# Low-part score and gate products on all 128 rows, with the low part written into both partition halves

## Chip, cores and metric

One NeuronCore of one Trainium2 chip runs the whole program in one launch. The metric is the device time of a launch in microseconds (us); lower is better. Engines: TensorE (PE, with its weight loads as PEld), VectorE (DVE), ScalarE (ACT), GpSimd (POOL) and SyncE (SP), which issues the DMAs. A line number such as L341 is a line of the kernel before; in the changed kernel the same statements stand two to four lines higher.

## The reference, cut to what matters

A two-layer decoder trunk on 512 tokens of width 1024, all in float32. Each layer has a hybrid mixer, a cross-attention into 256 memory tokens and a SwiGLU FFN. The two places of the mixer that matter here are the scores of branches A and C and the gates of branch B:

```python
s = jnp.einsum('bqhcd,bkhcd->bhcqk', qblk, k)          # branch A: 4 heads x 2 components of 64
s = jnp.einsum('bpnqhd,bpnkhd->bpnhqk', qb, kk)        # branch C: 8 heads of 64
gates = jnp.einsum('bsnc,gncd->gbsnd', xb, gate_w)     # branch B: 16 blocks of 64 x 64, two gates
```

In each the contraction runs over 64 channels.

## The kernel before

The matrix products run in fp32r, a float32 that carries fewer bits in a product. So a tensor is split into a high part (a cast) and a low part (the tensor minus its high part), and a product becomes high x high + low x high + high x low, three matmuls. The main weight products (L810 to L812 and L839 to L841) do this with 128 x 512 moving columns and contraction over all 128 rows, 24 matmuls to a step.

For the 64-channel contractions the kernel stacks two of these products in one matmul. `rope_item` makes, for a pair of 64-channel components (rows 0 to 63 and 64 to 127 of one tile), a Q tile `st[:, c, :]` that holds component c's high part in **both** partition halves (its second half is copied by two DMAs, L583 and L584), and a K tile that holds the high part in component c's own half and the low part in the other half (L587, L588). One matmul over 128 rows (L340) thus gives Qhigh x Khigh + Qhigh x Klow. The Q low part `ql` is one [128, 512] tile with each component in its own half (L581, L582), and its product (L341) uses the 64 rows of that half alone. The gates of branch B (`b_item`) are built the same way: `xs` is the high part in both halves (DMAs of L519 and L520), `gws` holds high and low gate weights, L524 runs over 128 rows and L525 over 64 rows with the low part `xl` (made on POOL, L517 and L518).

A layer has 4 head pairs in A and 4 in C. Each has one Q item and one K item of `rope_item`, and 4 query blocks of 128 queries; a query block has two score groups, each L340 then L341, whose moving width is 128, 256, 384 or 512. A layer has 8 gate items n = 0 to 7, each with two products of L524 and two of L525.

The order of the work is the order in which the program is written out: the loop at the end of the kernel emits one main step after another. Before each step `advance` moves every waiting generator (`rope_item`, `attn_a`, `attn_c`, `b_item`, `gelu_item`) on to its next `yield`, and `refill` and `flush` issue the casts and subtractions (L267 on ACT, L274 mostly on DVE) that split weight chunks needed some steps later. Every engine works its queue in that order, so an instruction that waits holds back all that is behind it on its engine. In layer 2 the four A heads follow one another as consecutive steps; in layer 1 two heads stand ahead of the V product and two behind it. Weight chunks, high and low parts share a pool of [128, 1024] tiles (`a4`, 39 buffers); [128, 512] tiles share `t2` (16 buffers).

Of the kernel before, what the change touches and what calls it, by code (L numbers as in the profile page):

```python
# [12 lines left out]
F32R = mybir.dt.float32r  # L13
AF = mybir.ActivationFunctionType
ALU = mybir.AluOpType
AX = mybir.AxisListType

P = 128
D = 1024
S = 512  # L20
# [33 lines left out]


def make_program():
    """Order of the matrix products: the weight chunks and the steps that use them.

    A chunk is [128, 1024] floats: (weight, layer, first row tile, row tiles, first column, columns).
    """  # L60
    chunks, steps = [], []

    def ch(name, l, k0, nk, c0, nc_):
# [3 lines left out]
    def tile_step(name, l, c0, act, post, n0=0, n1=S, **kw):  # L67
        c = ch(name, l, 0, KT, c0, P)
        st = Step("a", [c], act=act, post=post, nk=KT, ncol=P, off=0, n0=n0, n1=n1, **kw)
        steps.append(st)  # L70
        return st
# [11 lines left out]
    for l in range(L):  # L83
# [39 lines left out]
        for n in range(KT):  # L123
            st = tile_step("w_in", l, OFF_RX + P * n, "x", ("rx", l, n))
# [49 lines left out]
def kernel(  # L174
# [13 lines left out]
    nc = tc.nc  # L188
    chunks, steps = make_program()
# [3 lines left out]
    big = ctx.enter_context(tc.tile_pool(name="big", bufs=1))  # L193
# [4 lines left out]
    def nm(s):  # L198
        count[0] += 1
        return "%s_%d" % (s, count[0])  # L200

    def a4(s, shape, dt=F32):
        return big.tile([P] + shape, dt, tag="a4", name=nm(s), bufs=39)

    def t2(s, width=S):
        return big.tile([P, width], F32, tag="t2", name=nm(s), bufs=16)

    def t2r(s):
        return big.tile([P, S], F32R, tag="t2", name=nm(s), bufs=16)

    def small(s):
        return big.tile([P, 16], F32, tag="sm", name=nm(s), bufs=24)
# [1 line left out]
    def bank(s="ps"):  # L214
        return psp.tile([P, 512], F32, tag="bank", name=nm(s), bufs=8)

    def f(ap):
        return ap.bitcast(F32)

    V, A, G, T = nc.vector, nc.scalar, nc.gpsimd, nc.tensor  # L220
# [115 lines left out]

    def scores(sc, qk, c, i, w):
        qh, ql, kk = qk
        r = slice(64 * c, 64 * c + 64)
        T.matmul(sc[:, :w], qh[:, c, i * P:(i + 1) * P], kk[:, c, :w], start=True, stop=False)  # L340
        T.matmul(sc[:, :w], ql[r, i * P:(i + 1) * P], kk[r, c, :w], start=False, stop=True)  # L341

    def attn_a(l, h, i, qk):
        w = (i + 1) * P
# [162 lines left out]
    def b_item(l, n):  # L507
        xc = bt.pop(("xc", n))
        u, w = slice(0, 64), slice(64, P)
        gws = acts["gw"][n // 4]  # L510
        yield
        xs = a4("xs", [2, S], F32R)
        A.copy(xs[u, 0, :], xc[u])
        A.copy(xs[w, 1, :], xc[w])
        yield
        xl = t2r("xl")
        G.tensor_tensor(xl[u], xc[u], f(xs[u, 0, :]), ALU.subtract)  # L517
        G.tensor_tensor(xl[w], xc[w], f(xs[w, 1, :]), ALU.subtract)  # L518
        nc.sync.dma_start(f(xs[w, 0, :]), f(xs[u, 0, :]))  # L519
        nc.sync.dma_start(f(xs[u, 1, :]), f(xs[w, 1, :]))  # L520
        yield
        z = [bank("z0"), bank("z1")]
        for b, r in enumerate((u, w)):
            T.matmul(z[b], gws[:, n % 4, b, :], xs[:, b, :], start=True, stop=False)  # L524
            T.matmul(z[b], gws[r, n % 4, b, :], xl[r], start=False, stop=True)  # L525
        tr, ti = t2("tr"), t2("ti")
        A.activation(tr[u], z[0][u], AF.Tanh, scale=0.5, bias=hb[u, l, n:n + 1])
        A.activation(ti[u], z[0][w], AF.Tanh, scale=0.5, bias=hb[w, l, n:n + 1])
        A.activation(tr[w], z[1][w], AF.Tanh, scale=0.5, bias=hb[w, l, 8 + n:9 + n])
        A.activation(ti[w], z[1][u], AF.Tanh, scale=0.5, bias=hb[u, l, 8 + n:9 + n])  # L530
        yield
        if n % 2 == 0:
            bt["m"] = a4("m", [2, S])
        mp = bt["m"]
        a, m = t2("a"), mp[:, n % 2, :]
        A.activation(a, tr, AF.Exp, scale=nsp4[:, l, n:n + 1], bias=nsp4[:, l, n:n + 1])
        A.activation(tr, tr, AF.Tanh, scale=sp4[:, l, n:n + 1], bias=sp4[:, l, n:n + 1])
        A.activation(m, a, AF.Square)
        V.scalar_tensor_tensor(ti, ti, 1.0, xc, ALU.add, ALU.mult)
        yield  # L540
        V.scalar_tensor_tensor(m, m, 1.0, tr, ALU.add, ALU.mult)
        bt[("s", n)] = (a, ti, m)
        if n % 2 == 0:
            return
        yield
        A.activation(mp, mp, AF.Sqrt, scale=0.25)
        yield
        for k in (n - 1, n):
            a, ti, m = bt[("s", k)]
            G.tensor_tensor(ti, ti, m, ALU.mult)  # L550
        yield
        for k in (n - 1, n):
            a, ti, m = bt.pop(("s", k))
            V.tensor_tensor_scan(m, a, ti, 0.0, ALU.mult, ALU.add)
            V.scalar_tensor_tensor(m, bt.pop(("ge", k)), 0.5, m, ALU.mult, ALU.mult)
            A.copy(act_of("oB", k)[0], m)
        yield
        for k, m in zip((n - 1, n), (mp[:, 0, :], mp[:, 1, :])):
            dh, dl = act_of("oB", k)
            G.tensor_tensor(dl, m, f(dh), ALU.subtract)  # L560
            mark("oB%d" % l)
# [3 lines left out]
    def rope_item(ps, l, br, h, which):  # L565
        raw, sh = t2("raw"), t2("sh")
        A.copy(raw, ps)  # L567
        V.stream_shuffle(sh, ps, [(j + 8) % 16 if j < 16 else j for j in range(32)])
        tab = acts["tabs", 0]
        G.tensor_tensor(raw, raw, tab[:, 0, :], ALU.mult)  # L570
        G.tensor_tensor(sh, sh, tab[:, 1, :], ALU.mult)
        yield
        st = a4("qk" + br, [2, S], F32R)
        a, b = slice(0, 64), slice(64, P)
        V.tensor_tensor(raw, raw, sh, ALU.add)
        A.copy(st[a, 0, :], raw[a])
        A.copy(st[b, 1, :], raw[b])
        yield
        if which == 0:
            ql = t2r("ql")  # L580
            V.tensor_tensor(ql[a], raw[a], f(st[a, 0, :]), ALU.subtract)  # L581
            V.tensor_tensor(ql[b], raw[b], f(st[b, 1, :]), ALU.subtract)  # L582
            nc.sync.dma_start(f(st[b, 0, :]), f(st[a, 0, :]))  # L583
            nc.sync.dma_start(f(st[a, 1, :]), f(st[b, 1, :]))  # L584
            store[br, h] = (st, ql)
            return
        V.tensor_tensor(st[b, 0, :], raw[a], f(st[a, 0, :]), ALU.subtract)  # L587
        V.tensor_tensor(st[a, 1, :], raw[b], f(st[b, 1, :]), ALU.subtract)  # L588
        qk = store.pop((br, h)) + (st,)
        if h == 0:  # L590
            new_act("o" + br, 4)
        make = attn_a if br == "A" else attn_c
        launch = [(br, make(l, h, i, qk)) for i in range(NT)]
        if done.get("v%s%d" % (br, l), 0) < NT:
            store.setdefault("wait" + br, []).extend(launch)
        else:
            arriving.extend(launch)
# [266 lines left out]
    for k in range(2):  # L864
        c = slice(512 * k, 512 * (k + 1))
        xh, xl = (t[:, k, :] for t in acts["x"][0])
# [157 lines left out]
```

## Time and profile before

| what | value |
|---|---|
| median of 3 runs | 2272.38 us (2271.61 to 2273.64) |
| span of the profiled execution | 2272.3 us |
| PE busy | 2238.5 us (99%) |
| PE weight loads busy | 1821.5 us (80%) |
| DVE busy | 1267.1 us (56%) |
| ACT busy | 898.3 us (40%) |
| POOL busy | 351.6 us (15%) |
| mean granted TensorE clock | 0.991 of full speed |

Matmuls are pipelined and the record of one is longer than the time until the next one starts, so 99% busy doesn't mean that PE is at its peak. What a matmul costs is read from start to start.

### The profile page before, as it was taken

The page shows a single profiled execution, that of the slowest core. Times are in us where ns is not written, and L with a number is a line of the kernel's source. Part 1 is how long each engine was busy: PE and PEld are TensorE (multiplying, and loading weights), DVE is VectorE, ACT ScalarE, POOL GpSimd, SP SyncE. Part 2 cuts the span into 40 slices and gives each one's busy share as a digit, 9 for nine tenths or more (in the row PEclk, how much of TensorE's full clock was granted, in tenths as well). Part 3 has the DMA queues.
Part 4 walks back from the last instruction along what each step waited for, and adds up shares of the span by engine and source line. Part 5 has one row for each costly group of instructions (what it writes and reads, how often), then busy time and mean ns, then how long its engine had stood idle before and what let it go on. Part 6 is the DMA issues. An engine that isn't in the chain of part 4 may idle for free.

```text
span 2272.3 us, 26789 instructions
## 1 busy us (share of the span) xinstructions
PE 2238.5 (99%) x10516; PEld 1821.5 (80%) x10516; DVE 1267.1 (56%) x2058; ACT 898.3 (40%) x1583; POOL 351.6 (15%) x238
## 2 busy tenths in 40 slices
PE   9999999999999999999999999999999999999998
PEld 7778777778888888888887777777788888888887
DVE  6656766646655743243566476666467457332434
ACT  5444466644244332122134445666432342221330
POOL 2202213320300300000022031133203003000000
PEclk9999999999999999999999999999999999999999
DMA  7122323234332222142231222232343323222321
GB/s 269 63 65 76 101 66 97 93 98 166 102 112 102 93 91 86 66 147 100 81 126 56 65 75 93 65 107 84 116 148 105 110 101 103 85 82 97 125 93 38
DMA packets 65278, 224.37 MB, mean 99 GB/s; under 512 B 7936, under 2 KB 7936, under 8 KB 65152
## 3 DMA queue, kind: packets, MB, share of 16 engines
q1 hardware_dynamic: 65152, 222.66, 29.5%
q8 instruction: 83, 1.36, 0.2%
q14 instruction: 43, 0.35, 0.0%
HBM read 212.14 MB, written 2.10 MB: 94 GB/s over the span
## 4 chain that ended last, share of the span: by engine, by line
PE 72%; issue 17%; DVE 5%; POOL 3%; ACT 2%; DMA 0%; SPq 0%; POOLq 0%; ACTq 0%
PE ps L810 17%; PE ps L811 17%; PE ps L812 17%; PE ps L839 5%; PE ps L841 5%; PE ps L840 5%; POOL wlo L274 2%; PE sc L341 2%; PE o L414 1%; PE sc L340 1%; DVE x L482 1%; POOL ln L477 1%; PE tp L408 1%; PE o L370 1%; ACT whi L267 1%
## 5 line engine op out<-in xcount | busy, mean ns | idle before, releaser
L810 PE MATMUL ps<-xh,whi 128*128 128x512 f32 (+1 forms) x1792 | 697.3, 389 | 2.9 <-ACT xh L868 1.7
L811 PE MATMUL ps<-xl,whi 128*128 128x512 f32 (+1 forms) x1792 | 689.1, 385 | 0.8 <-DVE xl L754 0.5
L812 PE MATMUL ps<-xh,wlo 128*128 128x512 f32 (+1 forms) x1792 | 688.2, 384 | 1.3 <-POOL wlo L274 1.3
L274 DVE TENSOR_TENSOR wlo<-raw,whi 128x1024 fp32r<-128x1024 f32 x347 | 447.3, 1303 | 47.7 <-ACT whi L267 40.2
L267 ACT CAST whi<-raw 128x1024 fp32r<-128x1024 f32 x371 | 382.7, 1046 | 148.9 <-PE ps L840 97.8
L810 PEld LDWEIGHTS ps<-xh,whi 128*128 128x128 f32 x1792 | 339.4, 189 | 80.7 <-issue 6.5
L812 PEld LDWEIGHTS ps<-xh,wlo 128*128 128x128 f32 x1792 | 339.2, 189 | 68.9 <-POOL wlo L274 2.1
L811 PEld LDWEIGHTS ps<-xl,whi 128*128 128x128 f32 x1792 | 339.5, 189 | 66.1 <-DVE xl L869 1.0
L477 POOL TENSOR_TENSOR ln<-ln,expo 128x1 f32<-128x1 f32 x24 | 34.4, 1434 | 1082.9 <-DVE ln L476 1082.9
L839 PE MATMUL ps<-whi,hh 128*128 128x512 f32 x352 | 137.1, 389 | 0.0
L841 PE MATMUL ps<-whi,hl 128*128 128x512 f32 x352 | 137.0, 389 | 0.0
L840 PE MATMUL ps<-wlo,hh 128*128 128x512 f32 x352 | 136.9, 389 | 0.0
L744 ACT CAST hh<-fg 128x512 fp32r<-128x512 f32 x44 | 27.3, 620 | 191.8 <-DVE fg L743 191.8
L501 ACT CAST xh<-tp 128x256 fp32r<-128x256 f32 x80 | 28.0, 376 | 178.4 <-PE tp L495 101.2
L733 DVE SCALAR_TENSOR_TENSOR fg<-fg,ps 128x512 f32<-128x512 f32 x44 | 30.3, 688 | 116.9 <-ACT fg L732 116.9
L743 DVE TENSOR_TENSOR fg<-fg,ps 128x512 f32<-128x512 f32 x44 | 30.3, 688 | 114.4 <-PE ps L812 114.4
L570 POOL TENSOR_TENSOR raw<-raw,tabs 128x512 f32<-128x512 f32 x32 | 42.6, 1332 | 250.6 <-ACT raw L567 250.6
L732 ACT ACTIVATE fg<-ps 128x512 f32<-128x512 f32 x44 | 26.3, 598 | 135.2 <-PE ps L812 135.2
L680 DVE SCALAR_TENSOR_TENSOR x<-ps,x 128x512 f32<-128x512 f32 x48 | 33.0, 686 | 80.5 <-PE ps L841 80.4
L274 POOL TENSOR_TENSOR wlo<-raw,whi 128x1024 fp32r<-128x1024 f32 x24 | 63.5, 2661 | 88.4 <-ACT whi L267 88.4
L840 PEld LDWEIGHTS ps<-wlo,hh 128*128 128x128 f32 x352 | 66.1, 188 | 13.7
L839 PEld LDWEIGHTS ps<-whi,hh 128*128 128x128 f32 x352 | 66.1, 188 | 13.7
(233 smaller groups left out, 3576.6 us busy)
## 6 DMA issues: line engine op xcount, KB each, us to landing
raw<-in_wts_dram SPq DMA_DIRECT2D x371, 512.0 KB, 3.6
xs<-xs SPq DMA_DIRECT2D x32, 128.0 KB, 2.2
lng<-in_lnp_in_dram SPq DMA_DIRECT2D x6, 512.0 KB, 4.7
lnb<-in_lnp_in_dram SPq DMA_DIRECT2D x6, 512.0 KB, 5.0
tabs<-in_tabs_in_dram SPq DMA_DIRECT2D x4, 512.0 KB, 8.5
x<-in_x_in_dram SPq DMA_DIRECT2D x4, 512.0 KB, 9.3
qkA<-qkA SPq DMA_DIRECT2D x16, 128.0 KB, 2.2
qkC<-qkC SPq DMA_DIRECT2D x16, 128.0 KB, 2.2
```

The lines of the kernel that those rows point to most:

```text
L267: A.copy(h, raw)
L274: eng.tensor_tensor(lw, raw, f(h), ALU.subtract)
L341: T.matmul(sc[:, :w], ql[r, i * P:(i + 1) * P], kk[r, c, :w], start=False, stop=True)
L477: G.tensor_tensor(st[:, 15:16], st[:, 14:15], expo, ALU.pow)
L570: G.tensor_tensor(raw, raw, tab[:, 0, :], ALU.mult)
L680: V.scalar_tensor_tensor(xs, ps, co, xs, ALU.mult, ALU.add)
L810: T.matmul(pv, wh, xh, start=(kt == 0), stop=False)
L811: T.matmul(pv, wh, xl, start=False, stop=False)
L812: T.matmul(pv, wl, xh, start=False, stop=(kt == st.nk - 1))
L839: T.matmul(ps, xh, wh, start=(i == 0), stop=False)
L840: T.matmul(ps, xh, wl, start=False, stop=False)
L841: T.matmul(ps, xl, wh, start=False, stop=(i == n - 1))
```

## The change

The low parts get the layout of the high parts. `ql` and `xl` become [128, 2, 512] tiles of the `a4` pool, with each component's low part in both partition halves, and the second matmul of each pair (L341, L525) runs over all 128 rows, so that it also multiplies the low part with the low part of K or of the gate weight. The low parts are written with four subtractions of [64, 512] in place of two; those of `xl` move from POOL to DVE. The DMAs that copy the high part are now issued ahead of the subtractions in the program. The pool `a4` has 42 buffers, and a scratch area for dynamic DMAs is made smaller.

```diff
     def a4(s, shape, dt=F32):
-        return big.tile([P] + shape, dt, tag="a4", name=nm(s), bufs=39)
+        return big.tile([P] + shape, dt, tag="a4", name=nm(s), bufs=42)
...
     def scores(sc, qk, c, i, w):
         qh, ql, kk = qk
-        r = slice(64 * c, 64 * c + 64)
         T.matmul(sc[:, :w], qh[:, c, i * P:(i + 1) * P], kk[:, c, :w], start=True, stop=False)
-        T.matmul(sc[:, :w], ql[r, i * P:(i + 1) * P], kk[r, c, :w], start=False, stop=True)
+        T.matmul(sc[:, :w], ql[:, c, i * P:(i + 1) * P], kk[:, c, :w], start=False, stop=True)
...
-        xl = t2r("xl")
-        G.tensor_tensor(xl[u], xc[u], f(xs[u, 0, :]), ALU.subtract)
-        G.tensor_tensor(xl[w], xc[w], f(xs[w, 1, :]), ALU.subtract)
         nc.sync.dma_start(f(xs[w, 0, :]), f(xs[u, 0, :]))
         nc.sync.dma_start(f(xs[u, 1, :]), f(xs[w, 1, :]))
+        xl = a4("xl", [2, S], F32R)
+        for r in (u, w):
+            V.tensor_tensor(xl[r, 0, :], xc[u], f(xs[u, 0, :]), ALU.subtract)
+            V.tensor_tensor(xl[r, 1, :], xc[w], f(xs[w, 1, :]), ALU.subtract)
         yield
         z = [bank("z0"), bank("z1")]
-        for b, r in enumerate((u, w)):
+        for b in range(2):
             T.matmul(z[b], gws[:, n % 4, b, :], xs[:, b, :], start=True, stop=False)
-            T.matmul(z[b], gws[r, n % 4, b, :], xl[r], start=False, stop=True)
+            T.matmul(z[b], gws[:, n % 4, b, :], xl[:, b, :], start=False, stop=True)
...
         if which == 0:
-            ql = t2r("ql")
-            V.tensor_tensor(ql[a], raw[a], f(st[a, 0, :]), ALU.subtract)
-            V.tensor_tensor(ql[b], raw[b], f(st[b, 1, :]), ALU.subtract)
             nc.sync.dma_start(f(st[b, 0, :]), f(st[a, 0, :]))
             nc.sync.dma_start(f(st[a, 1, :]), f(st[b, 1, :]))
+            ql = a4("ql", [2, S], F32R)
+            for w in (a, b):
+                V.tensor_tensor(ql[w, 0, :], raw[a], f(st[a, 0, :]), ALU.subtract)
+                V.tensor_tensor(ql[w, 1, :], raw[b], f(st[b, 1, :]), ALU.subtract)
...
-    nc = _bacc.Bacc("TRN2", target_bir_lowering=False, num_devices=1)
+    nc = _bacc.Bacc("TRN2", target_bir_lowering=False, num_devices=1, dynamic_dma_scratch_size=2048)
```

On PE, ACT and SP the same instructions stand in the same order before and after; on PE the 160 matmuls that were 64 rows high are 128 rows high. DVE has 96 more instructions and POOL 32 fewer.

DVE in the A heads of layer 2, at the second Q item, before (the statement L575 that follows belongs to the K item of the same head, the L350 rows to the first query block of the first head):

```order
L568 STREAM_SHUFFLE sh_9127<-ps_9095 128x512
L581 TENSOR_TENSOR ql_9132<-raw_9033,qkA_9091 64x512
L582 TENSOR_TENSOR ql_9132<-raw_9033,qkA_9091 64x512
L575 TENSOR_TENSOR raw_9079<-raw_9079,sh_9080 128x512
L350 ISA pr_9142,st_9141<-sc_9144,tabs_8747 128x128
```

and after:

```order
L565 STREAM_SHUFFLE sh_9161<-ps_9129 128x512
L581 TENSOR_TENSOR ql_9168<-raw_9065,qkA_9125 64x512
L582 TENSOR_TENSOR ql_9168<-raw_9065,qkA_9125 64x512
L581 TENSOR_TENSOR ql_9168<-raw_9065,qkA_9125 64x512
L582 TENSOR_TENSOR ql_9168<-raw_9065,qkA_9125 64x512
L572 TENSOR_TENSOR raw_9113<-raw_9113,sh_9114 128x512
L346 ISA pr_9178,st_9177<-sc_9180,tabs_8779 128x128
```

Two more subtractions stand between the shuffle and the statement that releases ACT for the next item.

DVE at the first gate item (n = 0) of layer 1, before (here `oCl` is the low part of a C output, `pr` the probabilities of a C query block, `gq` the GELU argument):

```order
L419 TENSOR_TENSOR oCl_1788<-o_2614,oCh_1787 128x128
L400 RECIPROCAL st_2563<-st_2563 128x2
L402 TENSOR_SCALAR pr_2564<-pr_2564,st_2563 128x384
L402 TENSOR_SCALAR pr_2565<-pr_2565,st_2563 128x384
L661 TENSOR_SCALAR gq_2534<-gq_2534 128x512
L662 TENSOR_TENSOR gq_2534<-gq_2534,ps_2503 128x512
```

and after:

```order
L415 TENSOR_TENSOR oCl_1798<-o_2630,oCh_1797 128x128
L516 TENSOR_TENSOR xl_2647<-xc_2464,xs_2576 64x512
L517 TENSOR_TENSOR xl_2647<-xc_2464,xs_2576 64x512
L516 TENSOR_TENSOR xl_2647<-xc_2464,xs_2576 64x512
L517 TENSOR_TENSOR xl_2647<-xc_2464,xs_2576 64x512
L396 RECIPROCAL st_2579<-st_2579 128x2
L398 TENSOR_SCALAR pr_2580<-pr_2580,st_2579 128x384
L398 TENSOR_SCALAR pr_2581<-pr_2581,st_2579 128x384
L659 TENSOR_SCALAR gq_2550<-gq_2550 128x512
L660 TENSOR_TENSOR gq_2550<-gq_2550,ps_2519 128x512
```

The four `xl` subtractions stand ahead of the probabilities and of the GELU argument.

POOL at the last gate item (n = 7) of layer 1, before (`acc` is the merge of branch C, `bl` the low part of the B output):

```order
L550 TENSOR_TENSOR ti_3474<-ti_3474,m_3522 128x512
L550 TENSOR_TENSOR ti_3651<-ti_3651,m_3522 128x512
L631 TENSOR_TENSOR acc_2211<-acc_2211,g_3598 128x512 x2
L560 TENSOR_TENSOR bl_3340<-m_3522,bh_3339 128x512 x2
L517 TENSOR_TENSOR xl_3916<-xc_3809,xs_3874 64x512
L518 TENSOR_TENSOR xl_3916<-xc_3809,xs_3874 64x512
```

and DVE at the same item after:

```order
L628 SCALAR_TENSOR_TENSOR g_3624<-g_3624,ps_3925 128x512
L538 SCALAR_TENSOR_TENSOR m_3898<-m_3898,tr_3852 128x512
L516 TENSOR_TENSOR xl_3948<-xc_3839,xs_3904 64x512
L517 TENSOR_TENSOR xl_3948<-xc_3839,xs_3904 64x512
L516 TENSOR_TENSOR xl_3948<-xc_3839,xs_3904 64x512
L517 TENSOR_TENSOR xl_3948<-xc_3839,xs_3904 64x512
L659 TENSOR_SCALAR gq_3890<-gq_3890 128x512
```

Before, the `xl` of this item stood behind four additions of 128 x 512 on POOL; after, it stands on DVE ahead of the GELU argument.

## Rows read from the trace of the kernel before

**Rows 1.** The page: busy us (share) and instructions of each engine.

```profile
PE 2238.5 (99%) x10516; PEld 1821.5 (80%) x10516; DVE 1267.1 (56%) x2058; ACT 898.3 (40%) x1583; POOL 351.6 (15%) x238
```

**Rows 2.** PE in time, a score block 512 wide: start us, us, instruction.

```profile
296.19 0.47 PE L340 MATMUL sc<-qkC,qkC 128*128 128x512 f32 x1
296.60 0.50 PE L341 MATMUL sc<-qkC,ql 64*128 64x512 f32 x1
...
298.46 0.39 PE L812 MATMUL ps<-xh,wlo 128*128 128x512 f32 x1
298.68 0.40 PE L810 MATMUL ps<-xh,whi 128*128 128x512 f32 x1
```

**Rows 3.** PE in time, scores of cross-attention, 256 wide, all on 128 rows.

```profile
716.20 0.28 PE L429 MATMUL sc<-mkh,xqh 128*128 128x256 f32 x1
716.32 0.28 PE L430 MATMUL sc<-mkl,xqh 128*128 128x256 f32 x1
```

**Rows 4.** PE in time, a score block 128 wide (layer 1, A), with its wait.

```profile
89.28 0.55 PE L364 MATMUL tp<-ident,pr 128*128 128x128 f32 x3 [0.62 <-DVE pr L359]
89.58 0.31 PE L340 MATMUL sc<-qkA,qkA 128*128 128x128 f32 x1
...
91.15 0.40 PE L841 MATMUL ps<-whi,xl 128*128 128x512 f32 x1
```

**Rows 5.** PE in time, the gate products of one item.

```profile
304.14 0.50 PE L524 MATMUL z<-xs,gw 128*128 128x512 f32 x1
...
305.86 0.87 PE L408 MATMUL tp<-ident,pr 128*128 128x128 f32 x6
```

**Rows 6.** Lines 341 and 525: count, ns min/median/max, first and last start, forms.

```profile
L341 PE MATMUL sc<-qkA,ql x64: 323/408/686, 60.3 to 1308.0; 64*128 64x128 f32 x16, 64*128 64x256 f32 x16, 64*128 64x384 f32 x16, 64*128 64x512 f32 x16
...
L525 PE MATMUL z<-xl,gw x32: 491/498/792, 304.6 to 1600.5; 64*128 64x512 f32 x32
```

**Rows 7.** Waits of PE: who for whom, us in total, times, longest.

```profile
PE z L525 <- POOL xl L517: 5.4, 2, 2.7
...
PE tp L364 <- DVE pr L359: 4.4, 3, 3.3
...
PE ps L810 <- ACT ti L530: 1.2, 2, 0.6
```

**Rows 8.** PE in time at the last gate item of layer 1.

```profile
465.78 0.39 PE L524 MATMUL z<-xs,gw 128*128 128x512 f32 x1
468.89 0.79 PE L525 MATMUL z<-xl,gw 64*128 64x512 f32 x1 [2.72 <-POOL xl L517]
```

**Rows 9.** Stretches: length, busy us by engine, granted clock, DMA.

```profile
60.00:345.00 285.00, 283.77 (x1346) 218.48 (x1345) 183.81 (x442) 143.34 (x343) 58.10 (x48) 0.99 0.23 73
...
1202.00:1209.00 7.00, 6.86 (x16) 4.63 (x17) 4.94 (x11) 3.90 (x9) 2.41 (x2) 0.53 0.59 186
...
470.00:480.00 10.00, 10.00 (x32) 7.51 (x32) 1.92 (x2) 4.64 (x7) 0.18 (x1) 0.73 0.09 36
```

**Rows 10.** DVE in time, A heads of layer 2: the second Q item and the fourth.

```profile
1190.15 1.24 DVE L581 TENSOR_TENSOR ql<-raw,qkA 64x512 fp32r<-64x512 f32 x1
1191.41 1.68 DVE L582 TENSOR_TENSOR ql<-raw,qkA 64x512 fp32r<-64x512 f32 x1
...
1225.26 0.67 DVE L581 TENSOR_TENSOR ql<-raw,qkA 64x512 fp32r<-64x512 f32 x1
1225.94 0.69 DVE L582 TENSOR_TENSOR ql<-raw,qkA 64x512 fp32r<-64x512 f32 x1
```

**Rows 11.** POOL in time beside that second Q item.

```profile
1190.81 1.73 POOL L571 TENSOR_TENSOR sh<-sh,tabs 128x512 f32<-128x512 f32 x1
```

**Rows 12.** PE in time, the longest of its waits, layer 2, A.

```profile
1202.14 0.33 PE L364 MATMUL tp<-ident,pr 128*128 128x128 f32 x1 [3.29 <-DVE pr L359]
```

**Rows 13.** DVE, then ACT, in time around the first gate item of layer 1.

```profile
297.65 2.34 DVE L402 TENSOR_SCALAR pr<-pr,st 128x384 f32<-128x384 f32 x2
...
302.17 0.63 ACT L663 ACTIVATE gq<-gq 128x512 f32<-128x512 f32 x1 [4.40 <-DVE gq L662]
...
307.43 0.68 ACT L530 ACTIVATE ti<-z,hb 64x512 f32<-64x512 f32 x1
```

More of the change, by code (lines that the diff above doesn't have):

```diff
@@ L202, in a4 @@
     def a4(s, shape, dt=F32):
-        return big.tile([P] + shape, dt, tag="a4", name=nm(s), bufs=39)
+        return big.tile([P] + shape, dt, tag="a4", name=nm(s), bufs=42)
     def t2(s, width=S):
         return big.tile([P, width], F32, tag="t2", name=nm(s), bufs=16)
-    def t2r(s):
-        return big.tile([P, S], F32R, tag="t2", name=nm(s), bufs=16)
     def small(s):
```

## The prediction

> **What bounds the kernel now.** I read the shares of the engines first: PE is busy 2238.5 of 2272.3 us [rows 1], every other engine 56% or less. So time comes from what PE does between the start of one matmul and the next, and from the few places where it waits. In the list of its waits the largest are two of 2.7 us for `xl` from POOL, three that sum to 4.4 us for `pr` from DVE, and two of 0.6 us behind ACT's L530 [rows 7]. Then I read PE in time around the products that the change touches. The reader is to look at starts, not at durations: the next 128 x 512 main product starts 0.22 to 0.23 us after the last [rows 2], but the 64-row L341 starts 0.41 us after the 128-row L340 before it, and a whole block (four score products and the two main products behind them) takes from 296.19 to 298.46, 2.27 us, where six products at 0.23 would take 1.38 [rows 2]. Scores of cross-attention, which are alike but all 128 rows high, start 0.12 us apart at 256 columns [rows 3]. What differs is the height: at a change between 128 and 64 rows the next product starts only when the one before it is nearly through (0.41 us into a record of 0.47). There are 128 score products of 64 rows (line 341 has a second row like the one shown, for branch C) and 32 gate products [rows 6], each with one change into it and one out of it.
>
> **What the taller products give back.** A block 512 wide costs 2.27 - 1.38 = 0.89 us too much; four changes at 0.41 - 0.23 = 0.18 would be 0.72. Part of the first record's early start belongs to the transposes before it, and part of the delay falls on the main products behind, so I take 0.82, and the same for the widths of 384 and 256, whose changes are like it: 48 blocks, 39.4 us. A block 128 wide takes 91.15 - 89.58 = 1.57 us [rows 4]; with four products at the 0.12 of [rows 3] and two at 0.23 it would be 0.94. That is 0.63, and I take 0.58: 16 blocks, 9.3 us. The four gate products of an item take 305.86 - 304.14 = 1.72 us [rows 5] against 0.92, that is 0.80, and a little on what follows; 0.87 x 16 = 13.9 us. Together **62.6 us**, with 55 and 67 as ends (0.72 and 0.50 or 0.89 and 0.63 a block, 0.80 or 0.90 an item).
>
> On a rule against this: the Trainium skill, "TensorEngine Tiling (Array Packing)", section Performance Considerations, wants row tiling where the contraction is 64 or less, for up to twice the rate. By it a 64-row product would cost half of 0.23 at 512 columns, and the change would lose some 13 us over 160 products instead of giving 62.6. The trace speaks against that here: the 64-row product isn't beside another one but between two of 128 rows, and takes 0.43.
>
> **The wait for `xl`.** At gate item 7 of each layer L524 starts at 465.78 and L525 at 468.89 after a wait of 2.72 [rows 8], since `xl` stood behind four additions on POOL. In the ten microseconds from 470 the granted clock is 0.73 [rows 9], the lower level (1.2 GHz) for about half of them: 2.7 us more. The `xl` of that item now stands on DVE with none of POOL's work ahead of it, so I take the wait as gone: 2 x 5.4 = **10.8 us**, between 0 (the wait moves to DVE) and 10.8. The other moved `xl` cost POOL nothing that anybody waits for.
>
> **What the added subtractions cost.** Each of the 16 Q items has two more [64, 512] subtractions on DVE, each of the 16 gate items four. One takes 0.67 or 0.69 us alone and 1.24 or 1.68 beside POOL's two rope products [rows 10]. POOL is through at 1192.54 [rows 11] and the second subtraction 0.55 later, so the third and fourth should run alone: 1.36 us an item, with 2.92 as the other end. In most places this hides: from 60 to 345 DVE is busy for 184 of 285 us [rows 9]. It doesn't in three.
>
> *A heads of layer 2.* DVE and ACT hand work to each other here in a ring (shuffle, `ql`, L575, the casts, the next copy) that is slower than PE's steps, and PE ends up waiting 3.29 us [rows 12] and again for 0.5. All four Q items lie in that ring: 4 x 1.36 = 5.4 us later, and what PE saves before its last wait is swallowed by a longer wait: five score blocks, 2 x 0.58 + 3 x 0.82 = 3.6 us. So 9.0 us.
>
> *A heads of layer 1.* Two Q items lie in the same ring (the first of these waits is the 0.62 of [rows 4]): 2 x 1.36 + 3.6 = 6.3 us. That wait grows from 0.62 to about 4.5 us. Behind the 3.29 of layer 2 the clock fell to 0.53 for 7 us, which costs 3.3 [rows 9, 12]; half of it again here, since the next wait for DVE would swallow the rest: 1.6. The two A stretches give back **17 us**.
>
> *Gate item 0 of each layer.* The four `xl` subtractions (2.7 us) stand ahead of L402, which takes 2.34 for two beside POOL's work on the gate weights, and of L662, for which ACT waits 4.40 us before a queue that ends with L530, on which PE waits [rows 7, 13]. L402 will run faster when POOL is through, so I take 2.0 us, between 1.0 and 2.7. The wait of 0.6 then also swallows what PE saves since it last released DVE: a block of 512, the gate item and part of a block of 128, 2.1 us. With a dip of the clock for about 1 us that is 5 us a layer, **10 us**.
>
> The pool has three more buffers and takes the 32 extra tiles; the DMAs are the same ones in the same order, so I cost them at nothing: what hides them is that weights are split several steps ahead. If it fails, a late chunk stops PE; I leave that to the range.
>
> **The sum.** The profiled execution has a span of 2272.3, the median is 2272.38: the same. 2272.3 - 62.6 - 10.8 + 17 + 10 = **2226 us**.
>
> **The rivals.** (a) *Forecast*: 2212 to 2240, as the prices above move between their ends; chance 0.61. (b) *All of it is kept*: DVE's additions hide everywhere. 2272.3 - 62.6 - 10.8 = 2199, or 2194 to 2210 by the ends of the price. For it: DVE is idle for a third of the mixers [rows 9]. Against it: PE already waits for DVE in just the two A stretches [rows 7]. Chance 0.15. (c) *More is given back*: the moved subtractions also delay the weight splits (L274) and probabilities behind them in branch C and the gates, 15 to 30 us, and each longer wait brings the lower clock: 2241 to 2256. For it: ring-like waits as above; against it: `pr` and weights were otherwise ready microseconds early, since no other such wait is listed. Chance 0.15. (d) *The taller products don't help*: the weight load behind any score product is held back by something other than the height, such as the two products' common output bank. Then the 62.6 and the swallowed 3.6 and 2.1 fall away, and six Q items at 1.36, two gate items at 2.0 and the dips of the clock are left: 2272.3 - 10.8 + 8.2 + 4 + 3.6 = 2277, or 2273 without the dips: about the same. Against it: the products of [rows 3] share a bank too and start 0.12 apart. The Trainium skill, "TensorE: Matmul & The Clock Gate", Part 3, section The mechanism, says that a weight load overlaps running matmuls only where the row groups differ; by it full-height products would not overlap their loads either, and this case would hold. The trace disagrees with that rule already, as 0.12 us is less than the 0.28 of one such product. Chance 0.04. (e) *Slower*: DVE becomes the bound of both mixers. All 96 added subtractions (32 for `ql`, 64 for `xl`) at the mean price beside POOL, (1.24 + 1.68) / 2 = 1.46, are 140 us; once more than 52% of that reaches PE, the 73.4 us of gain are gone; if all does, 2272.3 - 73.4 + 140 = 2339. For it: DVE works in order, and a late subtraction holds everything behind it. Against it: even with 140 more, DVE would be busy 62% of the span, and most of the added work runs alone. Chance 0.05.
>
> **Numbers.** The likeliest is (a), 2226. The range 2205 to 2250 holds (a), the upper part of (b) and most of (c); outside stay about half of (b), a fifth of (c), (d) and (e), 0.2 in all. A difference of 0.2% (4.5 us) is about what a measurement here can tell from none. (a), (b) and (c) are faster: 0.91; (d) is the same: 0.04; (e) slower: 0.05.
>
> **What would show it.** In the profile after, L340 to L341 at 512 columns should start 0.23 apart, and a block should take 1.4 to 1.5 us instead of 2.27. The wait of L525 for `xl` should be gone and the clock near 470 full. The waits of L364 for `pr` should grow from 4.4 to 12 us or more in sum, with a clock below 1 near 90, and the wait behind L530 from 1.2 to about 8. DVE's busy time should rise by some 65 to 100 us, POOL's fall by about 50. If starts stay at 0.41 the first step is wrong and (d) holds; if the waits for DVE don't grow, it is (b); if new waits for `wlo` or `wT` stand in branch C or the gates, it is (c).

## The result, and the profile after

The changed kernel takes **2237.0 us** (2235.2 to 2237.6) against 2272.5 us before (2271.6 to 2273.6): a ratio of 0.984, interval 0.983 to 0.986. Its profiled execution has a span of 2233.4 us, 38.9 below the 2272.3 of before. The forecast was 2226, with a range of 2205 to 2250: the sign is right, the case is (a), and about a quarter of the forecast gain is missing (35.5 us by the medians, 38.9 by the spans, in place of 46.3).

The page's engines, to be set beside [rows 1] (busy us, share of the span, instructions):

```profile
PE 2180.9 (98%) x10516; PEld 1812.8 (81%) x10516; DVE 1318.1 (59%) x2154; ACT 893.2 (40%) x1583; POOL 300.9 (13%) x206
```

PE in time around the 512-wide block that [rows 2] show before (start us, duration us, line, operation, tiles, shape):

```profile
282.42 0.48 PE L336 MATMUL sc<-qkC,qkC 128*128 128x512 f32 x1
282.74 0.40 PE L337 MATMUL sc<-qkC,ql 128*128 128x512 f32 x1
282.97 0.39 PE L336 MATMUL sc<-qkC,qkC 128*128 128x512 f32 x1
283.20 0.39 PE L337 MATMUL sc<-qkC,ql 128*128 128x512 f32 x1
...
283.88 0.39 PE L810 MATMUL ps<-xh,wlo 128*128 128x512 f32 x1
```

From the first score product to the third main product behind the block it is 283.88 - 282.42 = 1.46 us, where it was 2.27 [rows 2]. From the second product on the starts are 0.23 apart, as forecast; the first gap, behind the transposes, is 0.32.

The list of PE's waits, which answers to [rows 7] (us in all, times, longest; L360 is L364 of before, L525 and L527 are L528 and L530, L522 is L525):

```profile
PE tp L360 <- DVE pr L355: 14.3, 6, 5.6
PE sc L336 <- ACT ti L525: 7.1, 4, 2.9
PE ps L810 <- POOL wlo L271: 5.0, 6, 1.9
...
PE ps L808 <- ACT ti L527: 2.8, 4, 0.7
PE tp L404 <- DVE st L390: 2.4, 2, 1.2
PE z L522 <- DVE xl L516: 1.6, 2, 0.8
```

The two waits of 2.7 for POOL are gone, but 0.8 for DVE stands in each one's place. The waits for `pr` grew from 4.4 to 14.3, and those behind the gates' tanh from 1.2 to 9.9, with 2.4 of a kind that wasn't there. The list of before has a line for `wlo` too, which [rows 7] leave out:

```profile
PE ps L812 <- POOL wlo L274: 5.1, 6, 1.9
```

So it is unchanged; its long waits lie behind the mixers (at 610 and 1740 us of before).

Granted clock at places that matter, in windows (us, then busy us and instructions of PE, PEld, DVE, ACT, POOL, then the clock, DMA share, GB/s; [rows 9] are of before):

```profile
290.00:300.00 10.00, 5.07 (x20) 3.60 (x18) 9.82 (x23) 7.58 (x18) 0.00 (x0) 0.77 0.16 52
300.00:310.00 10.00, 10.00 (x53) 8.13 (x52) 2.56 (x11) 5.36 (x11) 0.00 (x0) 0.89 0.00 0
446.00:456.00 10.00, 9.20 (x40) 7.00 (x39) 9.88 (x10) 3.49 (x6) 4.84 (x3) 1.00 0.76 250
456.00:466.00 10.00, 10.00 (x46) 8.29 (x45) 4.76 (x6) 8.09 (x11) 0.00 (x0) 1.00 0.39 127
1180.00:1190.00 10.00, 5.91 (x16) 4.99 (x17) 7.77 (x16) 3.91 (x9) 3.88 (x4) 0.66 0.34 92
```

Gate item 7 (446 to 466) runs at full clock now, as forecast. Gate item 0 (290 to 310) is the new trouble: PE is busy for half of 290 to 300, DVE for all of it. In the A heads of layer 2 (1180) PE waits 4 of 10 us.

**Where the time went.** PE runs the same instructions in the same order before and after, so the start of each can be compared with its own start before, and the difference assigned to stretches (before stands for one execution here, the profiled one). Outside the waits every block and item shows the same gain each time: 0.56, 0.78, 0.77 and 0.82 us for blocks 128, 256, 384 and 512 wide, 0.86 for a gate item, 16 of each, together 60.6. What a stretch lacks of that was given back. The next table is worked out in that way for the versions that keep PE's order, without `dma_low` (net change against before in the profiled executions, us, both layers; the experiments are told below):

| stretch | after | scores_only | gates_only | half_rows | zero_dve | after_gw_early | zero_gw_early |
|---|---|---|---|---|---|---|---|
| A heads with waits | +2.8 | +3.0 | -0.1 | +8.2 | -3.7 | +3.2 | -2.5 |
| other blocks of A and C | -32.8 | -32.8 | -0.1 | 0.0 | -32.8 | -32.8 | -32.8 |
| gate item 0 and block behind it | +10.3 | +6.8 | +5.6 | +6.3 | +2.8 | -0.5 | -2.4 |
| gate item 1 and block behind it | +0.6 | +0.1 | -0.3 | +0.4 | -0.3 | +0.5 | -0.3 |
| gate items 2 to 6 | -8.6 | 0.0 | -8.6 | 0.0 | -8.6 | -8.6 | -8.6 |
| gate item 7 | -10.2 | -1.5 | -10.1 | -9.7 | -12.9 | -10.2 | -12.9 |
| elsewhere | -1.2 | +1.0 | +0.9 | +1.2 | +2.4 | -0.3 | -1.7 |
| sum | -38.9 | -23.5 | -12.6 | +6.2 | -53.1 | -48.5 | -61.1 |

For the changed kernel: products 60.6, the wait for `xl` 8.4 (10.2 less the items' own 1.7), elsewhere 1.2; given back are 14.3 in the A heads, 13.1 at gate item 0 and 3.9 at gate item 1. 60.6 + 8.4 + 1.2 - 14.3 - 13.1 - 3.9 = 38.9.

**Gate item 0 in time.** DVE first, from the row after L415 (which starts at 284.75); [rows 13] are of before:

```profile
284.95 1.52 DVE L516 TENSOR_TENSOR xl<-xc,xs 64x512 fp32r<-64x512 f32 x1
286.49 1.69 DVE L517 TENSOR_TENSOR xl<-xc,xs 64x512 fp32r<-64x512 f32 x1
288.19 0.69 DVE L516 TENSOR_TENSOR xl<-xc,xs 64x512 fp32r<-64x512 f32 x1
288.91 0.69 DVE L517 TENSOR_TENSOR xl<-xc,xs 64x512 fp32r<-64x512 f32 x1
289.83 0.75 DVE L398 TENSOR_SCALAR pr<-pr,st 128x384 f32<-128x384 f32 x2
290.49 0.42 DVE L659 TENSOR_SCALAR gq<-gq 128x512 f32<-128x512 f32 x1
290.95 0.69 DVE L660 TENSOR_TENSOR gq<-gq,ps 128x512 f32<-128x512 f32 x1
```

Then ACT's first row behind it and the row that PE waits for, what POOL does at the time, and PE's two longest waits:

```profile
291.67 0.63 ACT L661 ACTIVATE gq<-gq 128x512 f32<-128x512 f32 x1 [6.41 <-DVE gq L660]
295.55 0.68 ACT L525 ACTIVATE ti<-z,hb 64x512 f32<-64x512 f32 x1
284.64 2.99 POOL L772 TENSOR_TENSOR gw<-gr,gw 64x512 fp32r<-64x512 f32 x2 [20.22 <-ACT gw L770]
292.30 0.55 PE L404 MATMUL tp<-ident,pr 128*128 128x128 f32 x3 [1.21 <-DVE st L390]
296.29 0.48 PE L336 MATMUL sc<-qkC,qkC 128*128 128x128 f32 x1 [2.94 <-ACT ti L525]
```

The reader is to see two things. The first two subtractions, beside POOL's split of the gate weights, take 1.5 and 1.7 us, the next two 0.69. And L398 and L659, which stood beside POOL before (as L402 and L661) and took 2.34 [rows 13] and 1.50, now come after it and take 0.75 and 0.42: POOL's slowing moved from one group of instructions to the other. ACT waits 6.41 us for L660, where it was 4.40, and PE, which comes earlier, waits 1.21 + 2.94 + 0.7 = 4.85.

### The profile page after: what moved, and what is told of

Read it like the earlier page. It is cut to its first block, busy times and chain, and to the rows that moved or that the text cites. A ratio compares the mean times of both kernels' runs of the same rounds, so it can differ in the third digit from the quotient of the medians.

```text
span 2233.4 us, 26831 instructions
## 1 busy us (share of the span) xinstructions
PE 2180.9 (98%) x10516; PEld 1812.8 (81%) x10516; DVE 1318.1 (59%) x2154; ACT 893.2 (40%) x1583; POOL 300.9 (13%) x206
## 3 DMA queue, kind: packets, MB, share of 16 engines
q8 instruction: 83, 1.36, 0.2%
## 4 chain that ended last, share of the span: by engine, by line
PE 69%; issue 17%; DVE 7%; ACT 3%; POOL 3%; DMA 0%; SPq 0%; POOLq 0%; ACTq 0%; DVEq 0%
PE ps L808 17%; PE ps L809 17%; PE ps L810 17%; PE ps L837 5%; PE ps L838 5%; PE ps L839 5%; POOL wlo L271 2%; PE o L410 1%; PE o L366 1%; DVE x L478 1%; POOL ln L473 1%; ACT whi L264 1%; DVE ql L582 1%; DVE xl L516 1%; PE sc L337 1%
## 5 line engine op out<-in xcount | busy, mean ns | idle before, releaser
L271 DVE TENSOR_TENSOR wlo<-raw,whi 128x1024 fp32r<-128x1024 f32 x347 | 441.9, 1287 | 40.3 <-ACT whi L264 36.5
L839 PEld LDWEIGHTS ps<-whi,hl 128*128 128x128 f32 x352 | 66.1, 188 | 13.7
```

The source lines that it names most:

```text
L271: eng.tensor_tensor(lw, raw, f(h), ALU.subtract)
L839: T.matmul(ps, xl, wh, start=False, stop=(i == n - 1))
```

## The experiments

My theory after the result (T): the height gives what the blocks show, wherever PE isn't waiting; what is lost is lost at stretches where PE waits for DVE and ACT anyway, partly to DVE's added subtractions and partly because PE only arrives earlier there. Rivals are named in each expectation.

**One half at a time.** `scores_only` keeps the change for scores and `ql`; `gates_only` for the gates and `xl`. The rest is as before:

```diff
 # scores_only
-            T.matmul(z[b], gws[:, n % 4, b, :], xl[:, b, :], start=False, stop=True)
+            T.matmul(z[b], gws[r, n % 4, b, :], xl[r], start=False, stop=True)
 # gates_only
-        T.matmul(sc[:, :w], ql[:, c, i * P:(i + 1) * P], kk[:, c, :w], start=False, stop=True)
+        T.matmul(sc[:, :w], ql[r, i * P:(i + 1) * P], kk[r, c, :w], start=False, stop=True)
```

> Only the 128 score products become 128 rows high (with the four subtractions of ql on DVE); the gates stay as before: xl by two subtractions on POOL, 64-row products. Theory (T): the price of a change of height is real everywhere, 46.8 us for the scores as the trace after has it block by block (16 x (0.56 + 0.78 + 0.77 + 0.82)); the A heads give back 14.3 as they did with the whole change, and what the first gate items give back (17.0 with the whole change) comes from xl on DVE, so here only what PE had saved before the wait is lost there, about 5 us. 2272.4 - 46.8 + 14.3 + 5 = 2245 us, the wait of the gate product for xl from POOL is back at 2.7 us or more, and the waits of the scores behind ti at gate item 0 are 1 us or less. Rival (R1): the gates give back 17 because PE is ahead there, whatever makes xl: 2272.4 - 46.8 + 14.3 + 17 = 2257 us.

> Only the 32 gate products become 128 rows high, with xl by four subtractions on DVE; scores and ql as before. Theory (T): the gates gain 16 x 0.86 = 13.8 and the wait for POOL's xl is replaced by one of 0.8 (8.4 in both layers); the four subtractions delay DVE by 2.0 at gate item 0, and with PE only 0.9 us further ahead there the waits are about 3.5 a layer, and nothing changes in the A heads: 2272.4 - 13.8 - 8.4 + 7 = 2257 us. Rival (R2): the whole 17.0 us that the first gate items gave back belong to these subtractions: 2272.4 - 22.2 + 17 = 2267 us.

Measured: `scores_only` 2250.8 us (ratio 0.990, interval 0.989 to 0.992), `gates_only` 2262.0 (0.995, 0.994 to 0.997). Both stand midway between the theory and its rival. The waits, of `scores_only` and then of `gates_only`:

```profile
PE tp L363 <- DVE pr L358: 14.3, 6, 5.6
PE z L524 <- POOL xl L516: 5.5, 2, 2.7
PE sc L339 <- ACT ti L527: 4.0, 2, 2.0
```

```profile
PE sc L339 <- ACT ti L529: 4.9, 2, 2.5
PE tp L364 <- DVE pr L359: 4.2, 3, 3.2
```

The A heads depend on the scores' part alone, as the theory had it (14.3 of waits with it, 4.2 without, against 4.4 before). But at gate item 0 either half alone brings waits of 2.0 or 2.5 behind `ti`, where the theory had 1 us or less for the scores alone: with `xl` still on POOL, PE's earlier arrival is enough, for DVE's chain is as long there as before (from L418 at 285.42 to the activation at 290.36, 4.9). So there both causes count, and neither the theory's split nor the rivals' was right.

**DVE's work without the height.** `half_rows` keeps tiles, subtractions and pool of the change, and reads only 64 rows:

```diff
-        T.matmul(sc[:, :w], ql[:, c, i * P:(i + 1) * P], kk[:, c, :w], start=False, stop=True)
+        r = slice(64 * c, 64 * c + 64)
+        T.matmul(sc[:, :w], ql[r, c, i * P:(i + 1) * P], kk[r, c, :w], start=False, stop=True)
-            T.matmul(z[b], gws[:, n % 4, b, :], xl[:, b, :], start=False, stop=True)
+            T.matmul(z[b], gws[r, n % 4, b, :], xl[r, b, :], start=False, stop=True)
```

> Everything of the change stays (tiles of 2 x 512, four subtractions for ql and xl on DVE, pool of 42), but the second score product and the second gate product read only the 64 rows of the component's own half, as before the change. Theory (T): the gain is in the height alone, so the 60.6 us are gone; the wait for POOL's xl is still gone (8.4), DVE's added work costs 6 Q items x 1.36 = 8.2 in the A heads and 2.0 at each first gate item, with some 3 for the clock: 2272.4 - 8.4 + 8.2 + 4 + 3 = 2279 us. Rival (R3): the give-back of 31 us after the change is the price of DVE's work alone: 2272.4 - 8.4 + 31 = 2295 us. Rival (R4): the layout and not the height gives the gain: about 2237 us.

Measured: 2281.4 us (1.004, 1.002 to 1.005): slower than before by 8.3. PE in time at the same 512-wide block:

```profile
299.90 0.47 PE L336 MATMUL sc<-qkC,qkC 128*128 128x512 f32 x1
300.30 0.50 PE L338 MATMUL sc<-qkC,ql 64*128 64x512 f32 x1
300.73 0.50 PE L336 MATMUL sc<-qkC,qkC 128*128 128x512 f32 x1
...
302.16 0.39 PE L811 MATMUL ps<-xh,wlo 128*128 128x512 f32 x1
```

The starts are 0.40 and 0.43 apart again and the block takes 2.26 us, so the height and not the layout gives the gain, and R4 is out. R3 (2295) is out too: DVE's work alone doesn't cost 31 us. The A heads are 8.2 us longer than before, which is 6 x 1.36: DVE's price as forecast, without what PE's arrival adds. In the steady blocks nothing changes (0.0 in the table): the new tiles, the bigger pool and the order of the DMAs cost nothing there.

**The height without DVE's work.** The other half of `ql` and `xl` need not hold a copy. If it holds zeros, the product adds nothing for it, and two subtractions are enough. `zero_dve` sets the off halves of three fixed tiles once:

```diff
+    def zinit(n):
+        for k in range(n):
+            t = cp.tile([P, 2, S], F32R, tag="zp%d" % k, name="zp%d" % k)
+            G.memset(f(t[64:P, 0, :]), 0.0)
+            G.memset(f(t[0:64, 1, :]), 0.0)
+            zpad.append(t)
...
-            ql = a4("ql", [2, S], F32R)
-            for w in (a, b):
-                V.tensor_tensor(ql[w, 0, :], raw[a], f(st[a, 0, :]), ALU.subtract)
-                V.tensor_tensor(ql[w, 1, :], raw[b], f(st[b, 1, :]), ALU.subtract)
+            ql = zp()
+            V.tensor_tensor(ql[a, 0, :], raw[a], f(st[a, 0, :]), ALU.subtract)
+            V.tensor_tensor(ql[b, 1, :], raw[b], f(st[b, 1, :]), ALU.subtract)
```

and likewise for `xl`, on DVE. The pool `a4` has 39 buffers again, to make room for the three tiles.

> 128-row products as after the change, but the half that holds a copy of the low part holds zeros instead: three fixed tiles whose off halves are set to zero once at the start, and two subtractions per Q item and per gate item (on DVE) in place of four. What is computed is that of the kernel before. Theory (T): the height gives 60.6 and the wait for xl is gone (10); the A heads lose only what PE saved before it met the ring (3.6 a layer, and some clock: 9), the first gate items DVE's 0.6, the old 0.6 and what PE saved (2.1), with some clock: 7.5. 2272.4 - 60.6 - 10 + 9 + 7.5 = 2218 us. Rival (R1): it is PE's being ahead that costs the 31 us, and DVE's added subtractions cost nothing: 2237 us, as after the change.

Measured: 2220.9 us (0.977, 0.976 to 0.979), 16 us below the change. Its waits:

```profile
PE tp L373 <- DVE pr L368: 10.3, 5, 4.3
PE sc L349 <- ACT ti L538: 4.2, 4, 1.9
```

The wait for `xl` is gone from the list, and gate item 7 gains 12.9 - 1.7 = 11.2 where the change gains 8.4. With no more work on DVE than before in the A heads, these still wait 10.3 us (4.4 before): that is PE's saving, swallowed. Rival R1 is out.

**Copies by DMA.** `dma_low` has two subtractions and two DMAs in place of four subtractions:

```diff
-                V.tensor_tensor(ql[w, 0, :], raw[a], f(st[a, 0, :]), ALU.subtract)
-                V.tensor_tensor(ql[w, 1, :], raw[b], f(st[b, 1, :]), ALU.subtract)
+            V.tensor_tensor(ql[a, 0, :], raw[a], f(st[a, 0, :]), ALU.subtract)
+            V.tensor_tensor(ql[b, 1, :], raw[b], f(st[b, 1, :]), ALU.subtract)
+            nc.sync.dma_start(f(ql[b, 0, :]), f(ql[a, 0, :]))
+            nc.sync.dma_start(f(ql[a, 1, :]), f(ql[b, 1, :]))
```

> The change with the copies of the low part made by DMA: two subtractions per Q item and per gate item on DVE, and two DMAs that copy the result into the other partition half, as the high part is copied. Theory (T): only DVE's time counts, and a copy of 2.2 us is hidden, since the products come a step later: as with zeros in the other half, 2221 us. Rival (R7): the low product at the gate items then waits for a copy that starts after the subtraction; at the first gate item of each layer by some 2 us and at the others not: 2225 us; if it waits at all 16 items by 1 us or more: 2237 us or more.

Measured: 2224.2 us (0.979, 0.977 to 0.980). One wait is new:

```profile
PE z L523 <- DMA xl<-xl: 2.0, 2, 1.0
```

It stands at gate item 7 of both layers, not at item 0 as R7 had it; elsewhere the copies are hidden, so the main theory holds, that it is DVE's time that counts. The time is nearer to R7's 2225 than to the theory's 2221.

**Gate item 0: the count of subtractions or POOL beside them.** Both `after_gw_early` (the change itself) and `zero_gw_early` (zeros in the other half) split the gate weights some six steps earlier; PE's and DVE's order stay:

```diff
         project("A", 4)
+        steps[-1].pre = ("gw", l, 0)
         project("A", 6)
+        steps[-1].pre = ("gw", l, 1)
...
-            if n < 2:
-                st.pre = ("gw", l, n)
```

> The version with zeros in the other half, and the gate weights of a layer split some six steps earlier (on the two projection steps ahead of the last C head), so that POOL's two subtractions on them no longer run beside DVE's work at gate item 0. Theory (T): those subtractions then take 0.69 in place of 1.7 and the probabilities and the GELU argument stay at 0.4 each, so the queue that ends in the release of the bank is 1.5 to 2 us shorter; the wait there falls from 2.9 to about 1 a layer and the dip of the clock behind it mostly goes: 2221 - 2 x 2.5 = 2216 us. Rival (R8): the wait at gate item 0 is set by the length of ACT's own queue (four tanh of 0.68 and the casts) and not by what DVE does before: 2221 us.

> The changed kernel with its four subtractions for xl and ql, and the gate weights of a layer split on the two projection steps ahead of the last C head, so that POOL no longer works beside DVE at gate item 0. It tells apart what the number of subtractions costs there and what their running beside POOL costs. Theory (T): four subtractions alone are 2.8 us in place of 4.6 (1.52 + 1.69 + 0.69 + 0.69), so the three waits at gate item 0 fall from 4.8 to about 3 us a layer and the dip of the clock behind them gets shorter: 2237 - 2 x 3 = 2231 us. Rival (R9): it is the number that counts, since four subtractions alone are as long as two beside POOL, and then this version ends where zeros with the late split ended at the gates: 2237 - 2 x 4 = 2229 or less; the waits at gate item 0 would be 2.9 a layer. Rival (R10): POOL's part is nothing here: 2237 us and waits of 4.8.

Measured: `zero_gw_early` 2213.4 us (0.974, 0.973 to 0.976), `after_gw_early` 2227.6 (0.980, 0.978 to 0.982). DVE at gate item 0 and the waits of `after_gw_early`:

```profile
284.15 0.67 DVE L516 TENSOR_TENSOR xl<-xc,xs 64x512 fp32r<-64x512 f32 x1
284.84 0.69 DVE L517 TENSOR_TENSOR xl<-xc,xs 64x512 fp32r<-64x512 f32 x1
...
286.25 0.69 DVE L517 TENSOR_TENSOR xl<-xc,xs 64x512 fp32r<-64x512 f32 x1
```

```profile
PE sc L336 <- ACT ti L525: 3.4, 4, 1.1
PE ps L808 <- ACT ti L527: 3.3, 4, 1.0
```

The subtractions beside POOL took 1.5 and 1.7, now 0.67 and 0.69. At gate item 0 PE waits 1.1 + 1.0 a layer in place of 4.85, the 2.4 for `st` are gone, and the granted clock stays full there. That is 9.4 us of the whole time with the same number of subtractions, more than the theory had (6); R10 is out. R9's time came true (2229 or less), and neither it nor the theory had the waits, which both put at about 3 a layer: the subtractions got 1.8 us shorter, and the waits fell by 2.8. What rules R9 out is the comparison of four versions in the table. At gate item 0 the early split takes 10.8 us off the change (10.3 to -0.5), and two subtractions in place of four take off 7.5 (10.3 to 2.8) with the late split but only 1.9 (-0.5 to -2.4) with the early one. So the two are not separate terms: the loss needs many subtractions and POOL beside them, and moving POOL is worth more. In `zero_gw_early` the item gives back next to nothing, and R8 is out:

```profile
PE sc L349 <- ACT ti L538: 0.7, 4, 0.2
```

It is the fastest version here: 59 us below before, 24 below the change.

**What the price is paid for.** `pairs_64` is the kernel before with the four score products of a block in the order high, high, low, low:

```diff
+        for c in range(2):
+            T.matmul(sc[c][:, :w], qh[:, c, i * P:(i + 1) * P], kk[:, c, :w], start=True, stop=False)
+        for c in range(2):
+            r = slice(64 * c, 64 * c + 64)
+            T.matmul(sc[c][:, :w], ql[r, i * P:(i + 1) * P], kk[r, c, :w], start=False, stop=True)
```

> The kernel before with one thing changed: the four score products of a query block stand as high, high, low, low (both 128-row products of the two components, then both 64-row ones, which use different halves of the rows and different banks) in place of high, low, high, low. The number of changes between 128 and 64 rows falls from four to two a block. Theory (T): the price is paid for each change of height, not by the 64-row product as such: half of the 46.8 us is saved, and some 6 us of that are swallowed at the waits for DVE and ACT: 2272.4 - 23.4 + 6 = 2255 us. Rival (R5): the 64-row product itself is slow, whatever its neighbour: 2272 us. Rival (R6), by the rule of the Trainium skill that two short products on different row groups run side by side: the second 64-row product is free too, about 0.15 us more for each of 64 blocks: 2245 us.

Measured: 2252.7 us (0.991, 0.990 to 0.993), 20.1 below before with no work added anywhere. PE at the 512-wide block (x2 is two instructions in one row):

```profile
285.54 0.71 PE L340 MATMUL sc<-qkC,qkC 128*128 128x512 f32 x2
286.18 0.51 PE L343 MATMUL sc<-qkC,ql 64*128 64x512 f32 x2
...
287.19 0.39 PE L814 MATMUL ps<-xh,wlo 128*128 128x512 f32 x1
```

The two 64-row products together fill 0.51 us, where one fills 0.50 in `half_rows`: they run side by side. The block takes 287.19 - 285.54 = 1.65 us. From the 1.46 of the full rows that is one product less and two changes of height more: 1.46 - 0.23 + 2 x 0.21. Before, four changes made 2.27 - 1.46 = 0.81, 0.20 each; in blocks 128 wide it is 0.56, or 0.14 each. So the price per change (T) and the running side by side (R6) are both there: over all widths the blocks gain 32.0 us (16 x (0.33 + 0.49 + 0.56 + 0.62), from starts), near R6's 33. Of these 12 are missing in the medians and 9 in the spans of the two profiles; the theory allowed 6 for the waits. R5 is out. The Trainium skill, "TensorEngine Tiling (Array Packing)", section Key Properties, says both that a change of the tiling mode drains TensorE and that tiles can load and multiply in parallel; this trace agrees that a change costs time, 0.14 to 0.2 us each, and that the two products run together; what TensorE does in the time of a change it doesn't show.

## Why the prediction was right in kind and 11 us off

*The height* (62.6 forecast, 60.6 measured): right. The block 512 wide saves 0.82 and the gate item 0.86, as taken; blocks 256 and 384 wide save 0.78 and 0.77, a little less than the 0.82 that I gave them, and 128 wide 0.56. Case (d) is out.

*The wait for `xl`* (10.8 forecast, 8.4 measured): the clock part came as read (full clock at 446 to 466), but "taken as gone" was too much: four subtractions on DVE still end 0.8 us late at gate item 7 of each layer, three of them beside POOL at 1.7 to 1.8 us each. With two it is gone (11.2 in `zero_dve`). The end at 0 was in the range; I took the other end.

*The A heads* (17 forecast, 14.3 measured): the mechanism holds, and in layer 2 its size (8.9, where I had 9.0); layer 1 gives back 5.5 where I had 7.9. `half_rows` gives DVE's 8.2 alone, `zero_dve` what PE's arrival swallows alone (7.8 of the 11.5 that the blocks there would save, where I had twice 3.6); together they would be 16.0, so the two overlap a little. PE and DVE in layer 2 of the change:

```profile
1184.09 0.47 PE L360 MATMUL tp<-ident,pr 128*128 128x128 f32 x1 [5.57 <-DVE pr L355]
1189.20 1.23 DVE L581 TENSOR_TENSOR ql<-raw,qkA 64x512 fp32r<-64x512 f32 x1
1190.44 1.68 DVE L582 TENSOR_TENSOR ql<-raw,qkA 64x512 fp32r<-64x512 f32 x1
1192.13 0.69 DVE L581 TENSOR_TENSOR ql<-raw,qkA 64x512 fp32r<-64x512 f32 x1
1192.84 0.69 DVE L582 TENSOR_TENSOR ql<-raw,qkA 64x512 fp32r<-64x512 f32 x1
```

The third and fourth subtraction run alone at 0.69, so 1.36 an item and not 2.92 was the right end. The waits in layer 1 are 1.6 and 2.4, 4.1 together. My figures didn't agree there: a wait that grows by 6.3 from 0.62 is 6.9 and not 4.5. The clock from 90 to 100 is 0.83, which costs 1.7 us, as taken (1.6).

*The gates* (10 forecast, 17.0 measured): **this is the term that failed.** Its first part stands: DVE's chain at gate item 0 grew by the 2.0 that I took (from the start of the low part of the C output to the activation that ACT waits for it was 302.17 - 297.25 = 4.9, it is 291.67 - 284.75 = 6.9), and the waits there are 4.85 a layer where 0.6 + 2.0 + 2.1 makes 4.7. Two parts were mis-sized. The lower clock behind that wait cost 1.8 us more than before in layer 1 and 2.8 in layer 2 (give-back of 6.06 and 7.07 less the 4.25 by which the waits grew), not 1. My working passed over that before had a dip there already, in layer 1 and not in layer 2 (1.00 from 1440 to 1450):

```profile
308.00:318.00 10.00, 9.83 (x47) 7.77 (x47) 3.47 (x10) 5.20 (x12) 0.00 (x0) 0.83 0.00 1
```

And gate item 1 was left out: PE, released at item 0, saves 0.56 + 0.78 + 0.77 + 0.86 = 3.0 us on its way to item 1 and waits there behind the same two lines of ACT, 0.6 and 0.7 us; 2.0 us a layer are lost (a listed wait counts from the end of the record before it; from start to start the two gaps are 0.99 and 1.07 us, where 0.23 is usual). The rule "a wait swallows what PE saves since the last release" was in my working, and I applied it to the waits that the profile of before listed and not to those that it would make.

*Pools and DMAs at nothing*: right by `half_rows` in the steady blocks. *DVE's busy time*: forecast to rise by 65 to 100, it rose by 51. The added subtractions alone are 76, as forecast; but other instructions of DVE that had run beside POOL took 24 less, above all the scaling L661 (15.4 to 6.8), L541 (17.6 to 11.0) and the weight splits L274 (about 5). POOL's fell by 51, as forecast. Case (c) had its chance in the right direction, but no wait for `wlo` or `wT` grew. Against (c) I said that no wait for weights is listed: the line for `wlo` above is, with 5.1 us one of the largest. It lies behind the mixers, so nothing came of the slip.

*Span and median taken as equal*: this is the rest, 3.4 us (38.9 by the spans, 35.5 by the medians), and it lies in which executions were profiled, not in the change. Wherever both are on record, the time of a run is 1.7 to 2.2 us above the span of the same execution (2235.2 and 2233.4 for the profiled one of the change). By that a span of 2272.3 belongs to a time of about 2274.1 (an estimate, 2272.3 + 1.8): 1.6 above the median of before, while the profiled execution of the change is the quickest of its four, 1.8 below their median. Part of it can be seen. Behind a wait of 1.9 for `wlo`, far from the changed products, the clock dips in the profile of before and not in that of the change (the first row is of before, the second the same work after):

```profile
1740.00:1750.00 10.00, 9.87 (x70) 9.87 (x71) 4.76 (x11) 6.83 (x14) 9.30 (x5) 0.83 0.42 134
1702.00:1712.00 10.00, 9.19 (x77) 9.19 (x78) 5.20 (x10) 6.28 (x12) 9.31 (x5) 1.00 0.67 210
```

That is 1.4 us of "elsewhere" in the table which the change did not earn. Why a dip comes in one place and not in another like it stays open: in `zero_dve` the waits at gate item 0 are 1.9 and 1.0 in both layers, and the clock behind them is full in layer 1 and about 0.7 for 6 us in layer 2.

## What to carry to other kernels

Here a product of 64 rows between products of 128 rows cost two changes of height of 0.14 to 0.2 us each. In such a place, fill the other half with zeros set once and run at full height, or set two such products on different halves side by side, before paying an engine for copies. When PE gets faster, go on along its path past the first wait: every place where it meets another engine's queue can become a wait, also those where it came late before and none is listed. And before costing an instruction added to DVE, look at what POOL does in that microsecond.

## What the runs showed of the hardware

- Two 64-row products on different halves of the rows and in different banks ran at the same time when they stood next to each other (0.51 us for both).
- A subtraction of [64, 512] on DVE takes 0.67 to 0.69 us alone and 1.5 to 1.7 beside subtractions of POOL; a scaling of [128, 384] 0.37 alone (0.75 for two) and 1.17 beside it [rows 13]. The Trainium skill, "SBUF — State Buffer", section "SBUF: two separate sides", says that DVE and POOL share one pair of ports, which an instruction holds as a whole; the trace agrees as far as DVE goes, which is slower by a factor of 2 to 3 here; POOL's own subtractions of the gate weights took 1.3 to 1.6 us each, and what DVE costs them no run here shows apart.
- Behind the waits of 4.85 us at gate item 0 of layer 1 the granted clock is 0.77 and then 0.89 over 10 us each, that is the lower of its two levels (1.2 and 2.4 GHz) for some 7 us ((2.3 + 1.1) / 0.5); behind those of 2.1 us in `after_gw_early` it stayed full. The length of the wait alone doesn't tell, for before, behind a wait of 0.60 there, it is 0.83 from 308 to 318.
